# The MLP of the last 1024 tokens as a 2x2 block product with seven products

## The chip, the cores and the metric

The kernel runs on one core of a Trainium2 chip. A core has TensorE (PE, the matrix unit), VectorE (DVE), ScalarE (ACT), GpSimd (POOL) and SyncE (SP). Here SP issues all data transfers (DMA) from one queue, in order; each engine takes its own instructions in order too, and waits for the others by semaphores. Operands lie in SBUF (128 partitions); TensorE adds up into PSUM, which has eight banks of 128x512 float32. The metric is the device time of one execution in microseconds, lower is better. Before the change it is 2673.2 us (median of 3 runs, 2673.03 to 2673.42).

## The reference

One layer on 2048 tokens of width 1024: two token mixers (attention and a state-space scan), a mixing projection that gives `h`, and then the MLP, which is all that the change touches:

```python
hn = rmsnorm(h, norm2_g)
a = jnp.square(jax.nn.relu(hn @ w_mlp_in.astype(jnp.float32)))   # 1024 -> 4096
h = h + a @ w_mlp_out.astype(jnp.float32)                        # 4096 -> 1024
```

## The kernel before

Tokens are kept reversed in time and cut into quarters of 512. Activations are kept with features on the partitions and tokens along the row, so a matmul has a 128x128 piece of a weight as its stationary operand and 128 features x 512 tokens as its moving one. Every float32 operand is split into a high part (rounded to the matmul's type `float32r`, a copy on ScalarE) and a low part (the difference, a subtraction on VectorE); `mm3` then issues three matmuls per pair: high x high, high x low, low x high. This splitting is the `split` of weights, activations and `hn`.

The program is a set of generators ("streams") that are run side by side, weighted by estimated cost; a scheduler then fixes the order of each engine's instructions when the program is built, with a model of its own for the times. The stages are: input projection and state space; attention; then for the quarters at tokens 1536 and 1024 the mixing projection and the MLP of that quarter (`mlp_stream` with 512 tokens, here called the quarter MLP); beside the second quarter MLP runs `mix_stream` for the last 1024 tokens in blocks of 256 ("mix2"), which writes `hS` (the residual) and `hnS` (the normed input, already split) to DRAM. The last stage is `mlp_stream` with 1024 tokens: this is the stage that is replaced.

In that stage, for each of the 32 chunks of 128 hidden features (`f`) and both halves of the tokens (`th`), `mlp1` makes 8 x 3 matmuls into one PSUM bank, ScalarE takes relu and square, VectorE splits the result, and the chunk's two halves wait as `a`. After each pair of chunks `mlp2` makes, for each of 8 output blocks and both token halves, 2 x 3 matmuls, and VectorE adds the bank to the residual `acc` in SBUF. Four `mlp2` units follow each `mlp1` unit. That is 64 times (24 + 24) = 3072 matmuls. `hn` and `acc` come from DRAM once; each chunk's `w1` and `w2` rows (512 KB each) are loaded and split once. After the last chunk each finished block of `acc` goes to `out`.

Of the kernel before, what the change touches and what calls it, by code (L numbers as in the profile page):

```python
# [31 lines left out]
for _n, _w in (("g1", 8), ("qg", 1), ("kg", 1), ("lre", 32), ("lim", 32), ("ldt", 32),  # L32
# [13 lines left out]
    "hnS": (2, 2, 128, 8, QT),  # L46
}

# [10 lines left out]
class Kern:  # L59
# [5 lines left out]
    # ---------------------------------------------------------------- helpers  # L65
# [18 lines left out]
    def mm3(self, ps, lh, ll, rh, rl, start, stop):  # L84
        mm = self.nc.tensor.matmul
        mm(ps, lh, rh, start=start, stop=False)  # L86
        mm(ps, lh, rl, start=False, stop=False)  # L87
        mm(ps, ll, rh, start=False, stop=stop)  # L88
# [9 lines left out]
    # ---------------------------------------------------------------- constants  # L98
# [18 lines left out]
    # ---------------------------------------------------------------- projection  # L117
# [174 lines left out]
    # ---------------------------------------------------------------- attention  # L292
# [155 lines left out]
    # ---------------------------------------------------------------- SSM parameters  # L448
# [62 lines left out]
    def ssm_params(self):  # L511
# [24 lines left out]
        # coefficient of b: (lam_bar - 1) / lam  # L536
# [18 lines left out]
        # powers of lam_bar, both orders  # L555
# [18 lines left out]
        # rho^8  # L574
# [4 lines left out]
        # signed unit phasors of 8 theta * 2^k  # L579
# [27 lines left out]
    # ---------------------------------------------------------------- SSM  # L607
# [8 lines left out]
    def ssm_stream(self):  # L616
# [15 lines left out]
        # phasor tables  # L632
# [46 lines left out]
        def tables(st, q):  # L679
# [21 lines left out]
            # input matrices  # L701
# [11 lines left out]
            # output matrices  # L713
# [142 lines left out]
    # ---------------------------------------------------------------- GLU, mixing, norms  # L856
# [155 lines left out]
    def mix_tail(self, X, b):  # L1012
# [23 lines left out]
    # ---------------------------------------------------------------- MLP  # L1036
    def mlp_stream(self, es, blocks, TB, p_hn, ps1, ps2, side="left", held=None):
# [3 lines left out]
        NT = TB // 512  # L1041
# [6 lines left out]
        p_acc = tp("acc", 1)  # L1048
# [13 lines left out]
        for t0 in blocks:  # L1062
            qs = list(range(t0 // QT, (t0 + TB) // QT))
            for q in qs:
                yield ("need", f"hn{q}")
            w1, w2, av, hn, acc = {}, {}, {}, {}, {}
            raw1 = {0: load("w1", 0)}
            for k in range(8):
                for x in range(2):
                    if held:  # L1070
                        hn[k, x] = held[0][k][:, x]
                        continue
                    t = p_hn.tile([128, TB], F32R, tag=f"hn{k}{x}", name=f"hn{k}{x}")
                    for i, q in enumerate(qs):
                        nc.sync.dma_start(out=t[:, i * QT:(i + 1) * QT].bitcast(F32), in_=S["hnS"][q, x, :, k, :])
                    hn[k, x] = t
            raw1[1] = load("w1", 1)
            w1[0] = split(raw1.pop(0), p_w1, "w1")
            raw2 = load("w2", 0)

            def mlp1(f, th):
                ps = ps1.tile([128, 512], F32, tag="m", name="m1")
                w = w1[f]
                sl = slice(th * 512, th * 512 + 512)
                for k in range(8):
                    self.mm3(ps, w[:, 0, k * 128:(k + 1) * 128], w[:, 1, k * 128:(k + 1) * 128],
                             hn[k, 0][:, sl], hn[k, 1][:, sl], k == 0, k == 7)
                r = p_r.tile([128, 512], F32, tag="r", name="r")
                nc.scalar.activation(out=r, in_=ps, func=ACTF.Relu)  # L1089
                nc.scalar.activation(out=r, in_=r, func=ACTF.Square)  # L1090
                if th == 0:
                    av[f] = p_a.tile([128, 2, TB], F32R, tag="a", name="a")
                a = av[f]
                nc.vector.tensor_copy(out=a[:, 0, sl], in_=r)
                tt(nc.vector, a[:, 1, sl], r, a[:, 0, sl].bitcast(F32), ALU.subtract)

            def mlp2(f0, o, th):
                ps = ps2.tile([128, 512], F32, tag="m", name="m2")
                sl = slice(th * 512, th * 512 + 512)
                for i in range(2):  # L1100
                    w, a = w2[f0 + i], av[f0 + i]
                    self.mm3(ps, w[:, 0, o * 128:(o + 1) * 128], w[:, 1, o * 128:(o + 1) * 128],
                             a[:, 0, sl], a[:, 1, sl], i == 0, i == 1)
                tt(nc.vector, acc[o][:, sl], acc[o][:, sl], ps, ALU.add)
# [175 lines left out]
```

## Time and profile before

| | |
|---|---|
| runs: median (lowest to highest) | 2673.2 us (2673.03 to 2673.42) |
| profiled execution: span from first to last instruction | 2671.6 us |
| last stage: first matmul on `hn` to end of the last matmul | 1958.5 to 2667.7 us |
| TensorE busy over the span | 2546.3 us (95%) |
| VectorE, ScalarE, GpSimd busy | 73%, 46%, 37% |
| mean granted TensorE clock | 0.978 |

The profiler recorded one execution; no time of its own for that execution beyond the span is shown, and the median of the runs is 1.6 us above the span. In the profile's rows, L73 is the helper that issues every two-operand elementwise operation, and L86 to L88 are the three matmuls of `mm3`. Matmuls are pipelined: a row's duration is about 0.39 us, while the next one starts about 0.23 us after it, so starts are what count. `x` is a count, and what stands behind the second bar is idle time ahead of the instructions and what ended it.

### The profile page before, as it was taken

To read this page: it belongs to the slowest core of one execution; us is meant where nothing else is said; L and a number is where in the kernel's file an instruction comes from. 1 tells how busy PE (TensorE), PEld (TensorE's weight loads), DVE (VectorE), ACT (ScalarE), POOL (GpSimd) and SP (SyncE) were. 2 spreads that over 40 slices of the span, in tenths; PEclk is the share of its full clock that TensorE was granted. 3 is DMA by queue.
4 is the path that set the end of the run, shared out by engine and by line. 5 is a ranking of instruction groups with operands and counts; after the bars stand their busy time and mean duration, and the time that the engine had idled before them with its cause. 6 is when DMAs were issued, how large, how long until landed. Compare 5 with 4: busy or idle time off the path is not lost.

```text
span 2671.6 us, 35510 instructions
## 1 busy us (share of the span) xinstructions
PE 2546.3 (95%) x12368; PEld 2096.5 (78%) x12368; DVE 1945.6 (73%) x2790; ACT 1216.8 (46%) x2193; POOL 990.3 (37%) x898
## 2 busy tenths in 40 slices
PE   8888889988899999999898999999999999999999
PEld 6776677876778888888686788888888888888887
DVE  7699997888998888988999876767644444444443
ACT  6444446765666566655665554444321121212120
POOL 5685766866865444544675312122000000000000
PEclk9999999999999999999998999999999999999999
DMA  8545448774443333333433355555651111111101
GB/s 290 189 122 158 134 147 245 201 211 122 140 122 108 120 116 104 120 108 105 135 108 98 101 174 164 196 190 170 236 189 40 55 40 56 40 56 40 56 26 70
DMA packets 247588, 340.66 MB, mean 128 GB/s; under 512 B 23280, under 2 KB 157168, under 8 KB 247408
## 3 DMA queue, kind: packets, MB, share of 16 engines
q1 hardware_dynamic: 247408, 338.38, 40.7%
q8 instruction: 98, 1.61, 0.2%
q14 instruction: 82, 0.67, 0.1%
HBM read 278.40 MB, written 58.72 MB: 126 GB/s over the span
## 4 chain that ended last, share of the span: by engine, by line
PE 68%; DVE 4%; issue 1%; ACT 1%; POOL 0%; DMA 0%; DVEq 0%; ACTq 0%; POOLq 0%
PE m L86 20%; PE m L88 20%; PE m L87 19%; PE at L389 3%; PE z L349 3%; PE o L409 2%; PE o L408 2%; DVE C L373 1%; DVE lo L73 1%; DVE h L73 1%; DVE w L73 0%; DVE hs L1023 0%; ACT s L364 0%; DMA w<-in_w_dram 0%; ACT a L365 0%
## 5 line engine op out<-in xcount | busy, mean ns | idle before, releaser
L73 POOL TENSOR_TENSOR a<-a,C 128x512 f32<-128x512 f32 (+1 forms) x320 | 463.7, 1459 | 362.3 <-DVE C L373 131.5
L73 DVE TENSOR_TENSOR acc<-acc,m 128x512 f32<-128x512 f32 x256 | 174.7, 684 | 391.0 <-PE m L88 387.2
L86 PE MATMUL m<-a,w 128*128 128x512 f32 x1024 | 402.9, 394 | 0.3 <-DVE h L73 0.3
L87 PE MATMUL m<-a,w 128*128 128x512 f32 x1024 | 399.6, 390 | 0.0
L88 PE MATMUL m<-a,w 128*128 128x512 f32 x1024 | 399.5, 392 | 0.0
L88 PE MATMUL m<-h,w 128*128 128x512 f32 (+1 forms) x992 | 357.3, 362 | 8.2 <-DVE w L73 8.1
L86 PE MATMUL m<-h,w 128*128 128x512 f32 (+1 forms) x992 | 358.8, 365 | 2.7 <-ACT w L905 1.4
L87 PE MATMUL m<-h,w 128*128 128x512 f32 (+1 forms) x992 | 358.0, 362 | 3.2 <-DVE h L73 3.1
L1089 ACT ACTIVATE r<-m 128x512 f32<-128x512 f32 x128 | 76.8, 600 | 599.3 <-PE m L88 599.1
L373 DVE TENSOR_TENSOR_SCAN C<-s,C,mz 128x513 f32<-128x513 f32 x192 | 273.5, 1440 | 15.2 <-ACT s L364 6.7
L73 DVE TENSOR_TENSOR w<-w,w 128x1024 fp32r<-128x1024 f32 x192 | 249.5, 1318 | 47.4 <-ACT w L1058 45.1
L364 ACT ACTIVATE s<-z 128x512 f32<-128x512 f32 (+1 forms) x320 | 172.2, 540 | 153.9 <-PE z L349 149.2
L1058 ACT ACTIVATE w<-w 128x1024 fp32r<-128x1024 f32 x192 | 198.8, 1057 | 91.3 <-PE m L88 68.5
L393 ACT ACTIVATE hi<-at 128x512 fp32r<-128x512 f32 (+1 forms) x320 | 170.3, 541 | 133.1 <-PE at L389 119.0
L88 PEld LDWEIGHTS m<-a,w 128*128 128x128 f32 x1024 | 192.2, 188 | 41.8
L86 PEld LDWEIGHTS m<-a,w 128*128 128x128 f32 x1024 | 192.3, 188 | 40.2 <-DVE h L73 0.9
L87 PE MATMUL m<-w,x 128*128 128x512 f32 x512 | 210.5, 411 | 13.9 <-DVE w L154 13.7
L87 PEld LDWEIGHTS m<-a,w 128*128 128x128 f32 x1024 | 192.4, 188 | 39.7
L86 PE MATMUL m<-w,x 128*128 128x512 f32 x512 | 209.5, 412 | 14.3 <-ACT w L153 7.4
L73 DVE TENSOR_TENSOR h<-h,m 128x512 f32<-128x512 f32 x256 | 170.2, 674 | 69.3 <-PE m L88 68.7
L73 DVE TENSOR_TENSOR lo<-at,hi 128x512 fp32r<-128x512 f32 (+1 forms) x320 | 185.3, 594 | 46.3 <-ACT hi L393 45.0
L88 PEld LDWEIGHTS m<-h,w 128*128 128x128 f32 x992 | 189.6, 191 | 37.1 <-DVE w L73 10.4
(211 smaller groups left out, 5418.4 us busy)
## 6 DMA issues: line engine op xcount, KB each, us to landing
w<-in_w_dram SPq DMA_DIRECT2D x192, 512.0 KB, 3.6
wr<-in_w_in_dram SPq DMA_DIRECT2D x104, 256.0 KB, 3.9
k<-kS SPq DMA_DIRECT2D x160, 128.0 KB, 3.5
v<-vS SPq DMA_DIRECT2D x80, 256.0 KB, 3.1
wr<-in_w_out_dram SPq DMA_DIRECT2D x40, 512.0 KB, 4.1
xr<-in_xt_dram SPq DMA_DIRECT2D x31, 512.0 KB, 4.3
xn<-in_xn_dram SPq DMA_DIRECT2D x16, 512.0 KB, 5.9
vS<-v SPq DMA_DIRECT2D x16, 512.0 KB, 4.1
```

The costliest lines, as they stand in the source:

```text
L73: eng.tensor_tensor(out=out, in0=a, in1=b, op=op)
L86: mm(ps, lh, rh, start=start, stop=False)
L87: mm(ps, lh, rl, start=False, stop=False)
L88: mm(ps, ll, rh, start=False, stop=stop)
L349: nc.tensor.matmul(z[:, i0:512], qt[g, h][m][:, u * 128:(u + 1) * 128], kt[b][:, i0:512], start=(m == 0), stop=(m == 1))
L364: nc.scalar.activation(out=s1[:, 1 + i0:513], in_=z[:, i0:512], func=ACTF.Sigmoid, scale=-0.125)
L373: nc.vector.tensor_tensor_scan(out=C[:, 0:513], data0=s1[:, 0:513], data1=self.mz[:, 128:641], initial=self.C[(n - 4) % 6][:, 512:513], op ...
L389: nc.tensor.transpose(at[:, u * 128:(u + 1) * 128], at_a[b, u][:, kb * 128:(kb + 1) * 128], self.ident)
L393: nc.scalar.activation(out=hi[:, :n], in_=at[:, :n], func=ACTF.Copy)
L408: nc.tensor.matmul(o[:, :n], vt[b][:, kb, :], hi[:, :n], start=first, stop=False)
L1058: nc.scalar.activation(out=w[:, 0], in_=raw, func=ACTF.Copy)
L1089: nc.scalar.activation(out=r, in_=ps, func=ACTF.Relu)
```

## The change

The last 1024 tokens are two blocks of 512 tokens. With features also cut in two, each of the two projections is a 2x2 block product, which is now made with seven block products (Strassen's method in Winograd's form) in place of eight. Both projections are no longer interleaved: all of the up projection comes first, its result goes through DRAM (`aS`), then the down projection.

- mix2 stores `hn` unsplit (one DMA in place of two, no split).
- `fast_types` makes the seven combinations of `hn` blocks (four plain differences or sums, three plain blocks) and splits them. Four of them (`TB11`, `TT1`, `TT2`, `TT3`) are made early, beside the end of the quarter MLP, in a pool on the right side of SBUF; three (`TB21`, `TB22`, `TT4`) when that MLP's memory is free.
- `fast_up` goes over 16 pairs of hidden chunks `i`. `fast_w1` loads four 128x512 pieces of `w1`, makes the four weight combinations and splits seven operands. Seven products of 4 x 3 matmuls go into three banks; some are added onto a bank that has been read already (`onto`). VectorE and ScalarE put the four results together, square them, and make the seven combinations for the down projection, which are stored unsplit in `aS`.
- `fast_down` goes product by product: seven products, each of 16 steps over the hidden chunks; a step makes 4 x 3 matmuls into four banks. Each step loads one 128x512 activation combination and one piece of `w2` (three pieces in the first product, `SS1`, which also makes `S2` on GpSimd and keeps it; none in the second, `SS2`), makes the weight combination where there is one, and splits both. The eight `f_raw` buffers take all of these loads. After a product's last step its banks are added to one or more blocks of the residual `C`, which is loaded from `hS` as four DMAs of 1 MB in the first step.

The core of the diff (removed text of `mlp_stream` for 1024 tokens and comment lines are left out):

```diff
-    "hnS": (2, 2, 128, 8, QT),
+    "hnS": (2, 128, 8, QT),
+    "aS": (7, 16, 128, QT),
...
-            h = self.split(X, hs)
-            hn.append(h)
-            if not X.held:
-                for x in range(2):
-                    nc.sync.dma_start(out=S["hnS"][Q, x, :, k, o0:o0 + TB], in_=h[:, x].bitcast(F32))
+            if X.held:
+                hn.append(self.split(X, hs))
+            else:
+                nc.sync.dma_start(out=S["hnS"][Q, :, k, o0:o0 + TB], in_=hs)
...
+    def hilo(self, pool, src, tag):
+        nc = self.nc
+        t = pool.tile([128, 2, 512], F32R, tag=tag, name=tag)
+        nc.scalar.activation(out=t[:, 0], in_=src, func=ACTF.Copy)
+        self.tt(nc.vector, t[:, 1], src, t[:, 0].bitcast(F32), ALU.subtract)
+        return t
...
+        for k in range(4):
+            if early:
+                b11, b12, b22 = load(0, k, "b11"), load(1, k, "b12"), load(1, k + 4, "b22")
+                t3 = stage.tile([128, 512], F32, tag="t3", name="t3")
+                self.tt(dve, t3, b22, b12, ALU.subtract)
+                self.tt(dve, b12, b12, b11, ALU.subtract)
+                keep(TB11, k, b11)
+                self.tt(dve, b22, b22, b12, ALU.subtract)
+                keep(TT1, k, b12)
+                keep(TT2, k, b22)
+                keep(TT3, k, t3)
+            else:
+                b21, b22 = load(0, k + 4, "b21"), load(1, k + 4, "b22")
+                keep(TB21, k, b21)
+                keep(TB22, k, b22)
+                t2 = ty[TT2, k].bitcast(F32)
+                t4 = stage.tile([128, 512], F32, tag="t4", name="t4")
+                self.tt(dve, t4, t2[:, 0], t2[:, 1], ALU.add)
+                self.tt(dve, t4, b21, t4, ALU.subtract)
+                keep(TT4, k, t4)
...
+            product(X, SA11, TB11, False)
+            p1 = out("p1")
+            nc.scalar.activation(out=p1, in_=X, func=ACTF.Copy)
...
+            product(Y, SS2, TT2, False)
+            u2 = out("u2")
+            tt(dve, u2, p1, Y, ALU.add)
...
+            product(Z, SS1, TT1, False)
...
+            product(Y, SS3, TT3, True)
+            u3 = out("u3")
+            tt(dve, u3, p1, Y, ALU.add)
+            v22 = out("v22")
+            tt(dve, v22, u3, Z, ALU.add)
+            nc.scalar.activation(out=v22, in_=v22, func=ACTF.Relu)
+            square(v22)
+            store(TB22, v22)
...
+            product(X, SA12, TB21, True)
...
+            product(Z, SS4, TB22, True)
...
+            product(Y, SA22, TT4, True)
...
+        order = [(SS1, TT1), (SS2, TT2), (SS3, TT3), (SS4, TB22), (SA11, TB11), (SA12, TB21), (SA22, TT4)]
...
+            if st == SS1:
+                a21, a22, a11 = quarter(i, 1, 0), quarter(i, 1, 1), quarter(i, 0, 0)
+                s1 = temp(a21, a22, ALU.add, "s1")
+                s2[i] = p_s2.tile([128, 512], F32, tag=f"s2_{i}", name="s2")
+                tt(nc.gpsimd, s2[i], s1, a11, ALU.subtract)
+                src = s1
+            elif st == SS2:
+                src = s2[i]
+            elif st == SS3:
+                src = temp(quarter(i, 1, 1), s2[i], ALU.subtract, "s3")
+            elif st == SS4:
+                src = temp(quarter(i, 0, 1), s2[i], ALU.subtract, "s4")
+            else:
+                src = quarter(i, *{SA11: (0, 0), SA12: (0, 1), SA22: (1, 1)}[st])
+            return self.hilo(self.f_hl, src, "hl")
...
+            prep(j + 1)
+            w, a = ready.pop((n, i))
+            for o in range(4):
+                c = slice(o * 128, (o + 1) * 128)
+                self.mm3(banks[o], w[:, 0, c], w[:, 1, c], a[:, 0], a[:, 1], i == 0, i == NP - 1)
+            if C is None:
+                C = {}
+                for th in range(2):
+                    for d in range(2):
+                        C[d, th] = p_h.tile([128, 4, 512], F32, tag=f"c{d}{th}", name="c")
+                        nc.sync.dma_start(out=C[d, th], in_=S["hS"][Q + th, :, 4 * d:4 * d + 4, :])
+                V = p_h.tile([128, 4, 512], F32, tag="v", name="v")
...
+                ps = (ps3, self.pool(el, "ps5b", 5, PSUM))
+                self.f_raw, self.f_hl = self.pool(el, "fraw", 8), self.pool(el, "fhl", 8)
+                self.f_s = self.pool(el, "fs", 1)
```

More of the change, by code (lines that the diff above doesn't have):

```diff
@@ L45 @@
     "hS": (2, 128, 8, QT),
-    "hnS": (2, 2, 128, 8, QT),
-}
+    "hnS": (2, 128, 8, QT),
+    "aS": (7, 16, 128, QT),
+}
+SA11, SA12, SA22, SS1, SS2, SS3, SS4 = range(7)
+TB11, TB21, TB22, TT1, TT2, TT3, TT4 = range(7)
 LN2_HI = 0.693359375
@@ L1034, in mix_tail, with mlp_stream @@
             self.flags.add(f"hn{Q}")
[L1037 removed]
+    def mlp_stream(self, es, t0, ps1, ps2, held, side="left"):
         nc, S, A = self.nc, self.S, self.A
@@ new lines, in mlp2 @@
+        def mlp2(f0, o):
+            ps = ps2.tile([128, 512], F32, tag="m", name="m2")
+            for i in range(2):
+                w, a = w2[f0 + i], av[f0 + i]
+                self.mm3(ps, w[:, 0, o * 128:(o + 1) * 128], w[:, 1, o * 128:(o + 1) * 128],
+                         a[:, 0], a[:, 1], i == 0, i == 1)
+            tt(nc.vector, acc[:, o, :], acc[:, o, :], ps, ALU.add)
+        todo = []
+        for f in range(NF):
+            if f + 2 < NF:
+                raw1[f + 2] = load("w1", f + 2)
+            if f + 1 < NF:
+                w1[f + 1] = split(raw1.pop(f + 1), p_w1, "w1")
+            mlp1(f)
+            yield mc
+            for _ in range(4):
+                if todo:
+                    mlp2(*todo.pop(0))
+                    yield mc / 4
+            w2[f] = split(raw2, p_w2, "w2")
+            if f + 1 < NF:
+                raw2 = load("w2", f + 1)
+            if f % 2 == 1:
+                todo = [(f - 1, o) for o in range(8)]
@@ new lines, in mlp_stream, with fast_types, load, keep @@
+        while todo:
+            f0, o = todo.pop(0)
+            mlp2(f0, o)
+            yield mc / 4
+            nc.sync.dma_start(out=self.out[o * 128:(o + 1) * 128, t0:t0 + 512], in_=acc[:, o, :])
+    def hilo(self, pool, src, tag):
[4 more added lines that the diff above has]
+        return t
+    def fast_types(self, stage, pool, early, ty):
+        nc, S = self.nc, self.S
+        dve = nc.vector
+        if early:
+            yield ("need", "hn1")
+            yield ("need", "hn0")
+        def load(half, k, n):
+            t = stage.tile([128, 512], F32, tag=n, name=n)
+            nc.sync.dma_start(out=t, in_=S["hnS"][half, :, k, :])
+            return t
+        def keep(t, k, src):
+            ty[t, k] = self.hilo(pool, src, f"ty{t}{k}")
+        for k in range(4):
+            if early:
+                b11, b12, b22 = load(0, k, "b11"), load(1, k, "b12"), load(1, k + 4, "b22")
[16 more added lines that the diff above has]
+                keep(TT4, k, t4)
+            yield 4.0
@@ new lines, in fast_w1, with load, temp @@
+    def fast_w1(self, i):
+        nc, A = self.nc, self.A
+        dve = nc.vector
+        def load(f, half, n):
+            t = self.f_raw.tile([128, 512], F32, tag="raw", name=n)
+            nc.sync.dma_start(out=t, in_=A["w1"][f, :, 4 * half:4 * half + 4, :].rearrange("p k t -> p (k t)"))
+            return t
+        def temp(a, b, op, n):
+            t = self.f_s.tile([128, 512], F32, tag=n, name=n)
+            self.tt(dve, t, a, b, op)
+            return t
+        hl = lambda src: self.hilo(self.f_hl, src, "hl")
+        a11, a21, a22, a12 = load(i, 0, "a11"), load(i + 16, 0, "a21"), load(i + 16, 1, "a22"), load(i, 1, "a12")
+        yield
+        w = {SA11: hl(a11)}
+        s1 = temp(a21, a22, ALU.add, "s1")
+        s2 = temp(s1, a11, ALU.subtract, "s2")
+        yield w
+        w[SS2] = hl(s2)
+        s3 = temp(a11, a21, ALU.subtract, "s3")
+        yield w
+        w[SS1] = hl(s1)
+        s4 = temp(a12, s2, ALU.subtract, "s4")
+        yield w
+        for t, src in ((SS3, s3), (SA12, a12), (SS4, s4), (SA22, a22)):
+            w[t] = hl(src)
+            yield w
```

264 lines of the change are left out of this document (176 added, 88 removed).

## The prediction

> **What bounds the kernel now.** I read the page first, for the span and the engines' shares, then the replaced stage alone: a table by windows, the chain of waits and the timeline.
>
> ```profile
> span 2671.6 us, 35510 instructions
> PE 2546.3 (95%) x12368; PEld 2096.5 (78%) x12368; DVE 1945.6 (73%) x2790; ACT 1216.8 (46%) x2193; POOL 990.3 (37%) x898
> ```
>
> The window row below lies inside the stage (length; busy time and count of PE, PEld, DVE, ACT, POOL; clock; DMA share; GB/s).
>
> ```profile
> 2008.86:2485.30 476.44, 476.44 (x2066) 387.17 (x2065) 203.57 (x301) 92.56 (x129) 0.00 (x0) 1.00 0.15 48
> ```
>
> TensorE is busy all of the time at full clock; VectorE 43%, ScalarE 19%, and DMA moves 48 GB/s. The stage is bound by its matmuls alone. Three pieces of the chain (start, length, what), one per 48 matmuls, give their rate:
>
> ```profile
> 2031.02 0.24 PE m L86
> 2042.10 0.24 PE m L86
> 2053.18 0.24 PE m L86
> ```
>
> The distance is 11.08 us, so 64 such parts take 64 x 11.08 = 709.1 us, or 230.8 ns per matmul. The timeline (start, length) has the stage's two ends and both kinds of matmul:
>
> ```profile
> 1958.54 0.40 PE L86 MATMUL m<-hn,w 128*128 128x512 f32 x1
> ...
> 2299.76 0.39 PE L87 MATMUL m<-a,w 128*128 128x512 f32 x1
> ...
> 2302.03 0.39 PE L88 MATMUL m<-a,w 128*128 128x512 f32 x1
> 2302.26 0.40 PE L86 MATMUL m<-hn,w 128*128 128x512 f32 x1
> ...
> 2305.99 0.39 PE L87 MATMUL m<-hn,w 128*128 128x512 f32 x1
> ...
> 2667.44 0.39 PE L88 MATMUL m<-a,w 128*128 128x512 f32 x1
> ...
> 2667.86 0.69 DVE L73 TENSOR_TENSOR acc<-acc,m 128x512 f32<-128x512 f32 x1 [0.67 <-PE m L88]
> ```
>
> From 1958.54 to 2667.67 are the same 709.1 us. Ten distances on `a` are 2.27 us, 227.0 ns each; sixteen on `hn` are 3.73 us, 233.1 ns each. Behind the last matmul lie one add and the last store, 3.8 us to the end of the span.
>
> **The change part by part: matmuls.** Up and down are 16 x 7 x 12 = 1344 matmuls each, 2688 in place of 3072. At 227.0 ns they take 610.2 us, at 233.1 ns 626.6 us. Why `hn` runs slower no row tells; it lies on the right side of SBUF, as the four early combinations do. I take 227.0 ns for 1920 matmuls and the middle, 230.1, for the 768 on early combinations: 435.8 + 176.7 = 612.5 us, 96.6 less than now. What remains is to count the waits that the new stage brings. It has 652 VectorE instructions (20 x 16 and 20 in up, 312 in down) where there were 448 (7 per 48 matmuls), and loads everything just ahead of use.
>
> Prices of one operation: groups of the stage (count, busy, mean ns, idle before), GpSimd's from the whole span, two VectorE rows that start 0.59 us apart, and transfers (count, KB, us to landing).
>
> ```profile
> L73 DVE TENSOR_TENSOR a<-r,a 128x512 fp32r<-128x512 f32 x59 | 40.6, 688 | 1.1
> L1090 ACT ACTIVATE r<-r 128x512 f32<-128x512 f32 x59 | 37.1, 628 | 1.0
> ```
>
> ```profile
> L73 POOL TENSOR_TENSOR a<-a,C 128x512 f32<-128x512 f32 x224 | 363.9, 1634 | 338.6 <-DVE C L373 131.5 <-ACT a L365 113.8 <-ACT s L364 16.8
> ```
>
> ```profile
> 1901.72 0.68 DVE L73 TENSOR_TENSOR h<-h,m 128x512 f32<-128x512 f32 x1
> 1902.31 0.68 DVE L73 TENSOR_TENSOR a<-r,a 128x512 fp32r<-128x512 f32 x1
> ```
>
> ```profile
> hn<-hnS SPq DMA_DIRECT2D x26, 256.0 KB, 6.0
> out_dram<-h SPq DMA_DIRECT2D x6, 256.0 KB, 3.3
> wr<-in_w_glu_dram SPq DMA_DIRECT2D x14, 256.0 KB, 2.9
> ```
>
> So a VectorE operation on 128x512 takes 0.69 us, or 0.60 in a row of independent ones; a high part on ScalarE 0.63; GpSimd's subtraction 1.63; a 256 KB load lands after 2.9 us, in a burst after 6.0.
>
> **Before the stage.** mix2 loses its split and one store of two. TensorE has no idle time there, so I cost the relief at nothing. Early combinations add 28 VectorE operations beside the quarter MLP:
>
> ```profile
> 1900.00:1957.00 57.00, 56.67 (x251) 46.60 (x250) 32.66 (x46) 14.02 (x18) 0.00 (x0) 1.00 0.71 255
> ```
>
> 32.7 + 28 x 0.60 = 49.5 of 57 us: covered, but that MLP has only three banks, and an add that stands behind others holds TensorE. 0 to 4 us; I take 1.
>
> **The opening.** On TensorE, before, the last matmuls of the quarter MLP (`m2`) are followed at once by those on `hn`:
>
> ```order
> L86 MATMUL m2_19927<-a_19826,w2_19861 128x512
> L87 MATMUL m2_19927<-a_19826,w2_19861 128x512
> L88 MATMUL m2_19927<-a_19826,w2_19861 128x512
> L86 MATMUL m1_20027<-hn00_19967,w1_20017 128x512
> L87 MATMUL m1_20027<-hn01_19970,w1_20017 128x512
> ```
>
> Now the same place (`fx`, `fy` banks, `ty` combinations, `hl` split weights):
>
> ```order
> L92 MATMUL m2_19884<-a_19783,w2_19818 128x512
> L90 MATMUL fx_20031<-ty00_18473,hl_19994 128x512
> L91 MATMUL fx_20031<-ty00_18473,hl_19994 128x512
> L90 MATMUL fy_20032<-ty40_18480,hl_20001 128x512
> L91 MATMUL fy_20032<-ty40_18480,hl_20001 128x512
> L92 MATMUL fx_20031<-ty00_18473,hl_19994 128x512
> ```
>
> Only two matmuls stand ahead of `hl_20001`. That tile lies where the quarter MLP's residual lay, so its high part waits for that residual's last add and store: 0.69 + 3.3 + 0.63 = 4.6 us, less two matmuls (0.45): 4.2 us idle. At least the four ScalarE copies queued there, 2.5 us; at most, with a store like a burst load, about 8.
>
> Does the gap slow the clock? One place shows it: rows of the timeline with the idle time before them, and windows after.
>
> ```profile
> 1429.17 1.12 PE L888 MATMUL m<-ident,rc 128*128 128x128 f32 x4 [3.55 <-POOL rc L73]
> ...
> 1436.58 0.44 PE L389 MATMUL at<-ident,a 128*128 128x128 f32 x2 [1.42 <-DVE lo L73]
> ```
>
> ```profile
> 1430.00:1434.00 4.00, 4.00 (x15) 3.33 (x14) 4.00 (x3) 2.29 (x5) 2.75 (x3) 0.50 0.22 89
> 1434.00:1438.00 4.00, 2.07 (x8) 1.03 (x7) 4.00 (x5) 3.98 (x8) 1.48 (x2) 0.93 0.47 131
> 1438.00:1442.00 4.00, 3.65 (x11) 3.06 (x12) 4.00 (x6) 1.68 (x5) 2.09 (x2) 0.59 0.15 33
> ```
>
> After 3.55 us the clock was 0.50 for 4 us, a loss of 2 us. Here 0 to 2; I take 1.
>
> **Up projection.** Late combinations are 20 more VectorE operations within the first two blocks: (20 + 40) x 0.60 = 36 us beside 168 matmuls of 38.8. Just covered; 0 to 5, I take 2. A later block has 20 VectorE operations (12.0 us), 16 on ScalarE (10) and 11 transfers of 256 KB beside 84 matmuls of 19.3 us. All hidden on average; but banks are written again after VectorE has read them, and a queue out of step costs up to one operation or two. 0 to 1 us per block; I take 0.25, so 4 us for 16.
>
> **From up to down.** On SP, the middle of the old stage held only weights:
>
> ```order
> L1053 DMA w1_20728<-in_w1_dram 128x1024
> L1053 DMA w1_20863<-in_w1_dram 128x1024
> L1053 DMA w2_20861<-in_w2_dram 128x1024
> L1053 DMA w2_20996<-in_w2_dram 128x1024
> L1053 DMA w1_20998<-in_w1_dram 128x1024
> ```
>
> At the turn of the new one stand the residual's four 1 MB loads, ahead of what step 2 of `SS1` needs (`ar_22630`, its activations):
>
> ```order
> L1223 DMA aS_65<-v11_22497 128x512
> L1350 DMA c_22608<-hS_63 128x2048
> L1350 DMA c_22610<-hS_63 128x2048
> L1350 DMA c_22612<-hS_63 128x2048
> L1350 DMA c_22614<-hS_63 128x2048
> L1320 DMA ar_22630<-aS_65 128x512
> L1293 DMA w2_22647<-in_w2_dram 128x512
> ```
>
> `c` takes memory of early combinations, which are free only near the end of up; from there to step 2 TensorE has 49 matmuls, 11.3 us. How fast loads go shows a window with a burst of `hn` loads, and the page's densest slice below that, its first:
>
> ```profile
> 1910.00:1920.00 10.00, 10.00 (x46) 8.29 (x45) 4.64 (x7) 1.22 (x2) 0.00 (x0) 1.00 1.04 388
> ```
>
> ```profile
> GB/s 290 189 122 158 134 147 245 201 211 122 140 122 108 120 116 104 120 108 105 135 108 98 101 174 164 196 190 170 236 189 40 55 40 56 40 56 40 56 26 70
> ```
>
> 4.19 MB at 388 GB/s are 10.8 us, then 2.9 for `ar` and 1.3 for its split: 15.0, so step 2 comes 3.7 us late (at 290 GB/s, 7.4; 0 if memory comes free early). The Trainium skill ("DMA: Bandwidth & Descriptors", Specifications) gives a core about 358 GB/s of HBM; by that the wait would be an estimated 4.6 us. The window of 388 speaks against it, and I go by the window.
>
> **Down projection.** A step is 12 matmuls, 2.76 us. VectorE's rows in `SS1` are per step (`s1` the combination, `hl` low parts), where the old stage had one add per 6 matmuls:
>
> ```order
> L77 TENSOR_TENSOR s1_22773<-w2_22767,w2_22769 128x512
> L77 TENSOR_TENSOR hl_22777<-s1_22773,hl_22777 128x512
> L77 TENSOR_TENSOR hl_22782<-ar_22780,hl_22782 128x512
> L77 TENSOR_TENSOR s1_22803<-w2_22797,w2_22799 128x512
> L77 TENSOR_TENSOR hl_22807<-s1_22803,hl_22807 128x512
> ```
>
> The second waits for ScalarE between: 0.69 + 0.63 + 0.60 + 0.60 = 2.5 us a step, just under TensorE, in `SS3` and `SS4` too (0 to 3 us, I take 0). `SS1` alone also loads 1.05 MB a step: 2.7 us at 388 GB/s, 3.6 at 290. With both so near I take 3.0: 13 steps x 0.24 = 3.1 us (0 to 11). The other products load half or a quarter of it, four steps ahead. At the products' ends 4 to 12 adds of 0.69 us stand between splits; the banks alternate, and 12 adds (8.3 us) with the splits of three steps (3.6) beside four steps (11) leave about 1 us late, as 8 do after `SS1`: 2 us together (0 to 5). The tail is the old one: four banks end 0.7 us apart, one add, one store.
>
> **Sum.** Waits: 1 + 4.2 + 1 + 2 + 4 + 3.7 + 3.1 + 2 = 21.0. Span: 2671.6 - 709.1 + 612.5 + 21.0 = 2596.0. The median lies 1.6 above the profiled span, so 2598 us, 75 less than 2673.2.
>
> **The rivals.** *Loads set the pace.* For: in a burst 256 KB landed after 6.0 us, and in `SS1` a buffer is used again every second step: 6.0 + 0.69 + 1.63 = 8.3 us per two steps, 4.2 a step, 13 x 1.4 = 18 in place of 3.1; with 1 us per block of up (16 for 4) and 7.4 for 3.7 that is 31 more: 2629. Against: `hn` kept 388 GB/s in such a burst.
>
> *Nothing waits but the opening.* 610.2 us of matmuls and 2.5: 2598 - 2.3 - 18.5 = 2577. For: VectorE's averages fit everywhere. Against: the order of loads at the turn.
>
> *Short waits keep the clock down, and it is slower.* If each step of down waits a little for a split, TensorE is never idle for long, yet the window at 1438 shows 0.59 after a gap of 1.42 us. Down's 1344 matmuls take 305 us at full clock; at a mean clock of 0.80 they take 76 more, which eats the whole gain; at 0.67, the mean of those three windows, 150 more: 2748. Against: no row of down's work is longer than a step, and the eight buffers let steps be made ahead. The Trainium skill ("TensorE: Matmul & The Clock Gate", the part on the clock gate) has the clock halved only after an idle window of about 3.4 us. By that rule, gaps of 1 us in each step change nothing; the 0.50 after 3.55 us agrees, the 0.59 after 1.42 does not.
>
> That the change doesn't do what it says is excluded for the matmuls: TensorE's rows are 384 fewer.
>
> **How the numbers follow.** Chances: forecast 0.76, loads 0.13, nothing waits 0.07, clock 0.04. The likeliest gives 2598. With every wait at its low end it is 2577, with every one at its high end (and 626.6 of matmuls) 2653; all at once is unlikely. From 2582 to 2634 lie the forecast and most of the loads case. 0.2% (5 us) is about what a measurement of this kernel tells from no change; only the clock case reaches beyond 2668, partly: faster 0.95, same 0.01, slower 0.04.
>
> **What would show it.** Right: the new stage about 634 us from the quarter MLP's last matmul; one idle time of some 4 us at the opening and one of 3 to 4 at step 2 of `SS1`; matmuls 227 to 233 ns apart; clock 1.00 but for these places. Wrong: idle time in every step of `SS1`, `SS3` or `SS4`, VectorE full in up, or a clock below 0.9 over a whole product.

## The result and the profile after

The changed kernel takes 2605.3 us (median of 4 runs, 2604.1 to 2611.1) against 2673.3 (4 runs): a ratio of 0.9749, 95% interval 0.9735 to 0.9763. The forecast was 2598 us, range 2582 to 2634: right side, inside the range, 7.3 us too low. The profiled execution is the longest of the four; its earlier stages ran some 4 us later than in a second profile of the same kernel (`after_again`, below), so the last stage is compared from its own first wait or its own start.

The page of the changed kernel, for the same two lines as before:

```profile
span 2609.4 us, 36346 instructions
PE 2471.2 (95%) x11984; PEld 2030.9 (78%) x11984; DVE 2069.8 (79%) x2990; ACT 1360.0 (52%) x2481; POOL 1023.4 (39%) x922
```

TensorE has 384 rows fewer and 75 us less of busy time; its share is still 95%, so the page alone does not tell that there is anything new to find. The windows do (length; busy time and count of PE, PEld, DVE, ACT, POOL; clock; DMA share; GB/s), from the opening to the turn into down:

```profile
1966.50:1970.80 4.30, 0.95 (x4) 0.36 (x3) 3.79 (x6) 2.45 (x6) 0.00 (x0) 1.00 0.66 209
1970.80:1974.40 3.60, 3.60 (x10) 2.78 (x11) 3.01 (x5) 3.60 (x8) 0.00 (x0) 0.55 0.34 116
2010.00:2280.00 270.00, 269.92 (x1167) 218.62 (x1166) 174.19 (x271) 126.70 (x222) 1.30 (x1) 1.00 0.44 151
2288.00:2292.00 4.00, 0.88 (x4) 0.38 (x3) 2.67 (x4) 0.01 (x1) 0.00 (x0) 1.00 0.95 342
2292.00:2296.00 4.00, 2.76 (x7) 2.21 (x8) 1.85 (x3) 1.26 (x2) 1.14 (x1) 0.50 1.03 389
2320.00:2330.00 10.00, 9.80 (x39) 6.50 (x38) 7.66 (x11) 3.58 (x6) 3.90 (x3) 1.00 0.99 337
```

Up (the third row) is solid: 1167 matmuls in 270 us, 231.4 ns each, nothing idle. Two short stretches stand almost empty, each with a stretch at half clock behind it. The last row, in `SS1`, is the one to look at twice: TensorE is "busy" 9.80 of 10 us, yet only 39 matmuls started, where 44 fit at 227 ns. A matmul's row is 0.39 us long and the next starts 0.23 us after it, so a start that slips by up to 0.16 us leaves no idle time. The count shows it; the busy share and the list of waits do not. That list, for TensorE from 1850 us on (total, times, longest):

```profile
PE g L90 <- ACT hl L1117: 7.7, 4, 4.4
PE m L90 <- DVE h L77: 2.8, 4, 1.4
PE fy L90 <- ACT hl L1117: 1.7, 1, 1.7
PE fx L90 <- ACT hl L1117: 1.6, 1, 1.6
PE g L91 <- DVE hl L77: 1.3, 1, 1.3
```

From the starts of all matmuls in the trace the stage divides as follows. "Free" is what the matmuls alone would take: 1344 x 231.4 ns in up, 227 ns in down; nine matmuls of `SS1` stand among the last ones of up, because the compiled order puts them there.

```
part                                       measured   free   more
last m2 to first fx                            1.99   0.23    1.8
first fx to last fz (up, 9 of SS1)           316.84  313.0    3.8
to the first matmul of SS2                    57.50   41.5   16.0
SS2                                           43.57   43.5    0.1
SS3 to the end of SA22                       219.17  217.6    1.6
stage                                        639.07  615.8   23.3
```

### The profile page after: what moved, and what is told of

Its sections match the earlier page's. It is cut to its first block, busy times and chain, and to the rows that moved or that the text cites. A ratio compares the mean times of both kernels' runs of the same rounds, so it can differ in the third digit from the quotient of the medians.

```text
span 2609.4 us, 36346 instructions
## 1 busy us (share of the span) xinstructions
PE 2471.2 (95%) x11984; PEld 2030.9 (78%) x11984; DVE 2069.8 (79%) x2990; ACT 1360.0 (52%) x2481; POOL 1023.4 (39%) x922
## 4 chain that ended last, share of the span: by engine, by line
PE 63%; DVE 6%; DMA 3%; issue 2%; ACT 1%; POOL 0%; SPq 0%; DVEq 0%; ACTq 0%; POOLq 0%
PE m L90 10%; PE m L92 10%; PE m L91 10%; PE g L91 3%; PE g L92 3%; PE z L353 3%; PE g L90 3%; PE at L393 3%; PE o L413 2%; PE o L412 2%; PE fy L90 2%; PE fy L91 2%; PE fy L92 2%; DVE C L377 1%; DMA w<-in_w_dram 1%
## 5 line engine op out<-in xcount | busy, mean ns | idle before, releaser
L91 PE MATMUL m<-w,x 128*128 128x512 f32 x512 | 210.9, 412 | 14.7 <-DVE w L158 14.5
L90 PE MATMUL m<-w,x 128*128 128x512 f32 x512 | 208.9, 411 | 14.8 <-DVE v L260 6.1
L90 PEld LDWEIGHTS m<-h,w 128*128 128x128 f32 x992 | 189.3, 191 | 34.9 <-ACT w L909 3.0
L92 PEld LDWEIGHTS m<-h,w 128*128 128x128 f32 x992 | 189.4, 191 | 34.3 <-DVE w L77 7.6
L91 PEld LDWEIGHTS m<-h,w 128*128 128x128 f32 x992 | 189.8, 192 | 29.7 <-DVE h L77 4.0
L92 PE MATMUL m<-w,x 128*128 128x512 f32 x512 | 208.3, 407 | 0.5 <-DVE x L77 0.5
L90 PE MATMUL m<-a,w 128*128 128x512 f32 x512 | 202.4, 396 | 2.2 <-DVE h L77 2.1
L91 PE MATMUL m<-a,w 128*128 128x512 f32 x512 | 200.4, 392 | 0.0
L92 PE MATMUL m<-a,w 128*128 128x512 f32 x512 | 200.1, 393 | 0.0
L77 DVE TENSOR_TENSOR w<-w,w 128x1024 fp32r<-128x1024 f32 x128 | 172.9, 1368 | 31.3 <-ACT w L1059 28.4
L77 POOL TENSOR_TENSOR s<-s,w 128x512 f32<-128x512 f32 x16 | 20.7, 1296 | 438.0 <-PE fx L92 376.3
L393 PE MATMUL at<-ident,a 128*128 128x128 f32 x1088 | 179.2, 281 | 4.6 <-POOL a L77 3.3
L91 PE MATMUL g<-hl 128*128 128x512 f32 x448 | 176.6, 394 | 1.9 <-DVE hl L77 1.3
```

What stands on the lines that cost most here:

```text
L77: eng.tensor_tensor(out=out, in0=a, in1=b, op=op)
L90: mm(ps, lh, rh, start=start, stop=False, skip_group_check=onto)
L91: mm(ps, lh, rl, start=False, stop=False, skip_group_check=onto)
L92: mm(ps, ll, rh, start=False, stop=stop, skip_group_check=onto)
L393: nc.tensor.transpose(at[:, u * 128:(u + 1) * 128], at_a[b, u][:, kb * 128:(kb + 1) * 128], self.ident)
```

## The experiments

The three questions: what the first 5.6 us cost, what makes `SS1` 16.0 us long, and why up's matmuls are slower than down's. Ratios are to the kernel before, with runs of it on the same chip; parts of the stage are counted as above.

### c_late: the residual's loads out of the turn

```diff
-            if C is None:
+            if n == 1 and i == 1:
                 C = {}
...
+                        tt(dve, C[d, th][:, 0, 0:1], s2[15][:, 0:1], s2[15][:, 0:1], ALU.add)
                         nc.sync.dma_start(out=C[d, th], in_=S["hS"][Q + th, :, 4 * d:4 * d + 4, :])
...
+            if n == 1 and i == 9:
+                for o in range(4):
+                    for d in range(2):
+                        tt(dve, C[d, 1][:, o, :], C[d, 1][:, o, :], held[o], ALU.add)
...
-                    add(C[0, 1])
-                    add(C[1, 1])
+                    held = banks
```

The small add in front of each load reads the last kept `s2`, so the load can't start before `SS1` has its operands; the banks of `SS1` are added to `C` in the tenth step of `SS2`.

> The residual's four 1 MB loads are held back until the last S2 of the first down product is made, and the first product's banks are added to it in the middle of the second product. If the bytes of these loads delay step 2 of the first product (my theory), the idle times of 4.4 and 1.6 us there and the low clock behind them (about 1.8 us) go: about 2598 us, 7 less than the changed kernel. Rival: step 2 waits for the store and load of its activations through DRAM or for SP's queue, whatever lies between: idle time as before, 2604 to 2606.

2600.9 us (2597.1 to 2603.9), ratio 0.9731 (0.9716 to 0.9746). In the changed kernel the turn read (SyncE's queue; start, length of the issue):

```profile
2277.91 2.08 SPq L1350 DMA_DIRECT2D c<-hS  x4
2280.08 0.53 SPq L1320 DMA_DIRECT2D ar<-aS  x1
```

```profile
c<-hS SPq DMA_DIRECT2D x4, 1024.0 KB, 8.8
```

```profile
2288.50 0.39 PE L92 MATMUL g<-hl 128*128 128x512 f32 x1
2293.24 0.80 PE L90 MATMUL g<-hl 128*128 128x512 f32 x1 [4.36 <-ACT hl L1117]
```

`ar`, the activations of a step, is issued behind the four `c` loads, which land after 8.8 us; TensorE stands still for 4.36 us. With the loads moved, the windows of the same times have no empty stretch and full clock:

```profile
2288.00:2292.00 4.00, 4.00 (x19) 3.30 (x19) 3.31 (x4) 1.15 (x2) 1.61 (x1) 1.00 1.05 399
2292.00:2296.00 4.00, 3.29 (x15) 2.26 (x13) 3.81 (x7) 1.11 (x2) 1.12 (x1) 1.00 0.99 344
```

The part up to `SS2` falls from 57.50 to 49.32 us: the loads' place costs 8.2 (7.6 against the 56.93 of the kernel's second profile). In the changed kernel these are the gap of 4.36, a second of 1.59 two steps later (its load stood behind stores of up's results), and twelve matmuls 0.43 us apart between them, at half clock, 2.4 us. The remaining 7.8 us over the free time are steps of 3.0 to 4.4 us in place of 2.72.

### s2_on_vector: S2 taken from GpSimd

```diff
-                tt(nc.gpsimd, s2[i], s1, a11, ALU.subtract)
+                tt(dve, s2[i], s1, a11, ALU.subtract)
```

> The first product's S2 is made on VectorE in place of GpSimd. If a step's 3.13 us there comes from the low part that takes 1.15 us beside GpSimd's subtraction (my theory), a step falls to 2.76 to 2.8 us, TensorE's own, though VectorE has one operation more: 13 x 0.35 = 4.6 us less, about 2600 us. Rival: the loads set it (1.05 MB per 3.13 us are 335 GB/s): steps stay at 3.1 us, 2605.

2603.1 us (2601.9 to 2612.4), ratio 0.9747 (0.9727 to 0.9768): the time hardly moves. The groups of `SS1` (2290 to 2340 us) in the changed kernel, then here:

```profile
L77 POOL TENSOR_TENSOR s<-s,w 128x512 f32<-128x512 f32 x13 | 16.8, 1295 | 35.6 <-DVE s L77 26.3 <-DMA aS<-v 9.3
L77 DVE TENSOR_TENSOR hl<-s,hl 128x512 fp32r<-128x512 f32 x13 | 15.1, 1161 | 10.1 <-ACT hl L1117 10.1
```

```profile
L77 DVE TENSOR_TENSOR hl<-s,hl 128x512 fp32r<-128x512 f32 x13 | 9.0, 692 | 0.6
L77 DVE TENSOR_TENSOR s<-w,w 128x512 f32<-128x512 f32 x13 | 9.0, 691 | 6.0 <-DMA w<-in_w_dram 5.9
```

The low part of the weight takes 692 ns in place of 1161 once GpSimd is idle, but then VectorE waits 5.9 us for `w`: another limit stands right behind the one removed.

### opening: other memory for the first split weights

```diff
-                self.f_raw, self.f_hl = self.pool(el, "fraw", 8), self.pool(el, "fhl", 8)
-                self.f_s = self.pool(el, "fs", 1)
+                self.f_hl, self.f_v = self.pool(el, "fhl", 8), self.pool(el, "fv", 1)
+                self.f_raw, self.f_s = self.pool(el, "fraw", 8), self.pool(el, "fs", 1)
                 with ExitStack() as eu:
-                    self.f_v = self.pool(eu, "fv", 1)
```

> The split weights get other memory, so that none lies where the quarter MLP's residual lay. If the second split weight waits for that residual's last store (my theory), the idle 3.4 us at the opening and about 1.8 us of low clock go: about 2600 us. Rival: the opening is bound by VectorE, which has the late combinations to split; the wait then moves a few us on, to the first late combination: 2604 to 2606.

2602.6 us (2600.9 to 2605.6), ratio 0.9742 (0.9725 to 0.9758). The changed kernel's opening, then this one's:

```profile
1966.27 0.39 PE L92 MATMUL m<-a,w 128*128 128x512 f32 x1
1968.26 0.50 PE L90 MATMUL fx<-ty,hl 128*128 128x512 f32 x1 [1.60 <-ACT hl L1117]
...
1970.74 0.50 PE L90 MATMUL fy<-ty,hl 128*128 128x512 f32 x1 [1.75 <-ACT hl L1117]
```

```profile
1958.98 0.39 PE L92 MATMUL m<-a,w 128*128 128x512 f32 x1
1959.20 0.40 PE L90 MATMUL fx<-ty,hl 128*128 128x512 f32 x1
```

The first matmul follows at once, which gives 1.8 us, and the second wait and the half clock are gone too. The two waits had different causes, which ScalarE's rows in the changed kernel show:

```profile
1966.02 1.15 ACT L1117 ACTIVATE ty<-b 128x512 fp32r<-128x512 f32 x2 [10.45 <-DVE h L77]
1967.07 0.61 ACT L1117 ACTIVATE ty<-t 128x512 fp32r<-128x512 f32 x1
1967.59 0.61 ACT L1117 ACTIVATE hl<-a 128x512 fp32r<-128x512 f32 x1
1970.06 1.67 ACT L1117 ACTIVATE hl<-s 128x512 fp32r<-128x512 f32 x3 [1.85 <-DVE t L77]
```

The first split weight (`hl<-a`) stood in ScalarE's queue behind three copies of late combinations (`ty`): that is the first wait. The edit also changed the compiled order: in `opening` this copy starts at 1948.19, ahead of them, so the first 1.8 us are the queue's and not shown to be the memory's. The second split weight (`hl<-s`) lies where the residual lay, and in the program its copy waits for the residual's last add, over at 1967.4, and for the stores, the last of which was issued at 1967.4 and landed 2.3 us later. (The row puts the wait down to a VectorE operation that ended at much the same time; the program has no such wait.) So the second wait was for that memory, as the prediction had it.

But up takes 0.4 us longer than before (317.28). Its first block of 84 matmuls is 3.7 us shorter (19.56 us), its second and fourth together 3.0 longer, its last 1.0 longer. VectorE, which has the late combinations to make, is full in the first block, as this window of `opening` shows, and TensorE waits for it in the second:

```profile
1959.20:1978.76 19.56, 19.56 (x85) 15.75 (x84) 19.56 (x34) 10.06 (x19) 0.00 (x0) 1.00 0.67 222
```

For this part the rival came: the second wait moved on to the late combinations. The stage is 2.9 us shorter: 1.8 less the 0.4, and another 1.6 that lie between up and `SS2`, where four steps behind a second gap of 2.84 us kept to 2.72 to 2.78 us; that part differs by 0.6 us between two runs of the changed kernel.

### fourth_matmul: are the products bound by their matmuls?

```diff
-                self.mm3(banks[o], w[:, 0, c], w[:, 1, c], a[:, 0], a[:, 1], i == 0, i == NP - 1)
+                self.mm3(banks[o], w[:, 0, c], w[:, 1, c], a[:, 0], a[:, 1], i == 0, i == NP - 1 and n < 4)
+                if n >= 4:
+                    nc.tensor.matmul(banks[o], w[:, 1, c], a[:, 1], start=False, stop=i == NP - 1)
```

Low x low is added in the last three products: 192 matmuls more.

> In the last three down products each step gets a fourth matmul per bank (low x low): 192 more matmuls and no more loads or splits. If matmuls set the pace there (my theory), 192 x 0.227 = 43.5 us more: about 2649 us. Rival: loads or splits set it and TensorE has room: at most 10 us more, 2615.

2647.7 us (2644.9 to 2649.7), ratio 0.9906 (0.9891 to 0.9921), 42.4 us above the changed kernel. In the trace the last five products take 261.1 in place of 219.2 us, 41.9 more; 192 x 226.7 ns are 43.5, less the 1.6 us that the changed kernel loses there at a product's end, which a longer step hides. So down behind `SS2` is bound by matmuls alone.

### late_and_opening, all_three and the control

`late_and_opening` has both edits, `all_three` also S2 on VectorE; `after_again` is the changed kernel once more, on the same chip.

> The four residual blocks are loaded in the second product in place of the first, SS1's own adds to them follow there, and the buffers of the high and low parts and of the results are taken from SBUF ahead of the raw ones at the opening. Counted from the first wait beside the quarter MLP to the last matmul, the late residual alone took 690.5 us and the opening alone 695.6, the changed kernel 698.7. If the two are separate costs they add up: about 687.4 us, a time about 11 us below the changed kernel where the run is free of drift, 2594 to 2599 us. Rival: what the opening gives is given back at the turn (its waits there were 4.04 and 2.84 us against 4.36 and 1.59), so that with the turn relieved only the late residual counts: 690.5 us, 2598 to 2601.

> As late_and_opening, and SS1's S2 is also made on VectorE in place of GpSimd. Theory: in SS1 two limits lie close together. With GpSimd busy, VectorE's subtraction hl<-s,hl takes 1.16 us in place of 0.69 and the step takes 3.13 us; without it, the steps wait for loads of w, but there the burst of the residual's loads still stood in the way. With both taken away, a step needs five VectorE operations (3.4 us at 0.69, but 3.0 at 0.60 in a row) and 1 MB of loads (2.7 us at 388 GB/s): between 2.8 and 3.1 us in place of 3.13, so 0 to 4 us below late_and_opening. Rival: the loads alone set 3.1 us at the 338 GB/s of this stretch, and nothing is gained.

> The changed kernel once more, on the same chip as the three others: 2605 us, and in its profile no late start of the last stage: from the first wait beside the quarter MLP to the last matmul 698.7 us as before, while that first wait comes at about 1902 us in place of 1906.45, if the 8 us that the stage began late in its first profile were a drift of that run.

```
                   us (lowest to highest)        ratio (95%)             stage   up     to SS2
after_again        2606.4 (2603.3 to 2609.0)   0.9744 (0.9731-0.9757)  639.03  316.93  56.93
late_and_opening   2594.8 (2591.8 to 2599.1)   0.9702 (0.9689-0.9715)  628.60  316.68  49.01
all_three          2596.6 (2591.2 to 2597.9)   0.9704 (0.9690-0.9717)  628.93  316.25  49.68
```

The control's stage is the same to 0.04 us and begins 4 us earlier than in the first profile: that lateness was the run's. The two costs are separate: the loads' place gives 8.2 us of the stage, the opening 2.3 on top of it; the medians lie 11.6 apart. From the first wait beside the quarter MLP to the last matmul `late_and_opening` takes 687.7 us, as expected. `all_three` gains nothing. VectorE there makes four operations a step (not the five of the expectation), and between 2295 and 2325 us it stood idle five times, 5.2 us in all, each time for a piece of `w`: the loads alone hold `SS1` as much as GpSimd does. Whether by their rate (318 GB/s there) or because a load starts only when VectorE has given a buffer back, no run separates.

### fewer_loads and a11_in_second: which limit holds SS1

Both stand on `late_and_opening`. `fewer_loads` leaves a load out and keeps GpSimd's operation (its `S2` is then another matrix); `a11_in_second` relieves both, with S1 kept and S2 made in `SS2`.

```diff
-                a21, a22, a11 = quarter(i, 1, 0), quarter(i, 1, 1), quarter(i, 0, 0)
+                a21, a22 = quarter(i, 1, 0), quarter(i, 1, 1)
+                a11 = a21
```

```diff
-                a21, a22, a11 = quarter(i, 1, 0), quarter(i, 1, 1), quarter(i, 0, 0)
-                s1 = temp(a21, a22, ALU.add, "s1")
                 s2[i] = p_s2.tile([128, 512], F32, tag=f"s2_{i}", name="s2")
-                tt(nc.gpsimd, s2[i], s1, a11, ALU.subtract)
-                src = s1
+                tt(dve, s2[i], quarter(i, 1, 0), quarter(i, 1, 1), ALU.add)
+                src = s2[i]
             elif st == SS2:
                 src = s2[i]
+                tt(dve, src, src, quarter(i, 0, 0), ALU.subtract)
```

> On top of late_and_opening: SS1's third load is left out and its second operand is taken from the first piece, so S2 and with it the output are others; GpSimd still makes S2. If GpSimd's work beside VectorE alone can hold SS1 at 3.1 us per step, the pace stays at 3.1 and hl<-s,hl at 1.1 us (687 us from the first wait to the last matmul). If the loads are what holds it, as in all_three, and VectorE's slower subtraction only fills idle time, the pace falls to 2.72 us (682 us).

> On top of late_and_opening: the third piece of w2 of each step is loaded in SS2 in place of SS1, and S2 is made there on VectorE, in place of the kept S1. SS1 then has three loads per step (768 KB) and three VectorE operations, SS2 two loads, and GpSimd has nothing. Theory: SS1's steps of 3.13 us had two limits close together, VectorE slowed by GpSimd's S2 and the loads of 1 MB per step; with both taken away its matmuls set the pace, 48 x 0.0567 = 2.72 us per step, and 13 steps give back 5.3 us: 682.4 us from the first wait beside the quarter MLP to the last matmul, against 687.7; 2589 to 2592 us. Rival: a third limit (ScalarE's copies in a chain with VectorE) keeps 3.1 us; or SS2, beside the loads of the residual, now waits in its turn: 687 us, no gain.

2591.9 us (2590.5 to 2599.3; 0.9698, 0.9679 to 0.9716) and 2595.5 (2591.4 to 2597.3; 0.9703, 0.9687 to 0.9720). The same ten microseconds of `SS1` in `late_and_opening`, `all_three`, `fewer_loads` and `a11_in_second`:

```profile
2310.00:2320.00 10.00, 9.76 (x40) 6.73 (x39) 7.30 (x10) 3.88 (x8) 4.38 (x4) 1.00 0.93 317
```

```profile
2310.00:2320.00 10.00, 8.33 (x36) 6.14 (x35) 8.25 (x13) 3.46 (x6) 0.00 (x0) 1.00 0.94 315
```

```profile
2310.00:2320.00 10.00, 9.81 (x40) 6.71 (x39) 7.66 (x10) 4.07 (x9) 4.10 (x4) 1.00 0.79 250
```

```profile
2310.00:2320.00 10.00, 10.00 (x46) 8.29 (x45) 7.76 (x16) 4.73 (x9) 0.00 (x0) 1.00 0.93 290
```

In the first two the pace is alike on the mean whichever engine makes S2, though not in these ten microseconds (40 and 36 matmuls): the steps from the fifth on take 3.3 and 3.4 us. With DMA down to 79% and GpSimd still at work there are 40 matmuls as before; these steps take 3.15 us, and the part up to `SS2` 46.93 in place of 49.01 (from the first wait beside the quarter MLP to the last matmul 685.7 us, between the two expected values). `a11_in_second` has the same three loads and the same three VectorE operations in a step of `SS1` and differs there by GpSimd's operation: so GpSimd alone can hold the pace, and the loads add a little. With both relieved there are 46 matmuls, every step of `SS1` but the first is 2.72 us, and the part up to `SS2` takes 43.07. The expected 5 us of gain still went elsewhere: at the end of up the compiled order has three matmuls of `SS1` in place of nine, and TensorE waited for `p` there:

```profile
2265.34 0.39 PE L92 MATMUL fy<-ty,hl 128*128 128x512 f32 x1
2267.80 0.50 PE L90 MATMUL fx<-ty,hl 128*128 128x512 f32 x1 [2.07 <-ACT p L1227]
```

Up grew from 316.7 to 318.9 with six matmuls fewer in it, and `SS2`, now with loads beside the residual's, from 43.5 to 45.9. The stage is 1.3 us shorter, the time the same: the rival's outcome, with the mechanism of the theory.

How GpSimd holds a step is seen in the changed kernel's timeline (VectorE, GpSimd):

```profile
2323.40 0.68 DVE L77 TENSOR_TENSOR s<-w,w 128x512 f32<-128x512 f32 x1
2324.86 1.15 DVE L77 TENSOR_TENSOR hl<-s,hl 128x512 fp32r<-128x512 f32 x1 [0.78 <-ACT hl L1117]
2325.93 0.68 DVE L77 TENSOR_TENSOR hl<-ar,hl 128x512 fp32r<-128x512 f32 x1
2326.53 0.68 DVE L77 TENSOR_TENSOR s<-w,w 128x512 f32<-128x512 f32 x1
...
```

```profile
2324.16 1.30 POOL L77 TENSOR_TENSOR s<-s,w 128x512 f32<-128x512 f32 x1 [1.83 <-DVE s L77]
```

GpSimd starts as soon as `s` is there and ends at 2325.46; VectorE's subtraction begins at 2324.86 and ends at 2326.01, 0.55 us behind GpSimd's end. The same 0.55 us come out in every step from 2305 us on, as if it got its turn only at that end. From one `s` to the next are 3.13 us. The Trainium skill ("SBUF — State Buffer", "SBUF: two separate sides") says that a VectorE operation with two SBUF inputs and a GpSimd operation that reads SBUF exclude each other for the whole instruction; this timing agrees. VectorE's adds from PSUM (`c<-c,g`) beside GpSimd's adds kept their 0.67 us.

### halves_in_turn: the waits beside the quarter MLP

On top of `a11_in_second`:

```diff
-                b11, b12, b22 = load(0, k, "b11"), load(1, k, "b12"), load(1, k + 4, "b22")
+                b12, b22, b11 = load(1, k, "b12"), load(1, k + 4, "b22"), load(0, k, "b11")
                 t3 = stage.tile([128, 512], F32, tag="t3", name="t3")
                 self.tt(dve, t3, b22, b12, ALU.subtract)
+                keep(TT3, k, t3)
...
-                keep(TT3, k, t3)
```

> a11_in_second, and the early combinations begin with those of the second token half (TT3), whose input was stored a block earlier; the ones that need the last block's stores come behind them. In the changed kernel ScalarE stood 10.06 us and VectorE 5.67 us for the first load of hn, with the quarter MLP's copies and adds queued behind, and TensorE lost 1.34 + 0.66 + 0.35 us. If the last store is what all waited for, these 2.4 us mostly go: about 2 us below a11_in_second. Rival: the wait only moves, since the operation on the last block still stands ahead of the MLP's on both engines: no difference that can be measured.

2595.8 us (2592.8 to 2600.6), ratio 0.9711 (0.9693 to 0.9730): the rival. Waits of TensorE there (1895 to 1920 us) in `after_again`, and here:

```profile
PE m L90 <- DVE h L77: 2.4, 3, 1.3
```

```profile
PE m L90 <- ACT r L1076: 1.7, 1, 1.7
PE m L90 <- DVE h L77: 0.4, 1, 0.4
```

The wait moved from VectorE's adds to ScalarE's copies; both queues still have a combination of the last block ahead of the MLP's work.

### act_right and act_left: does the place of the moving operand set its rate?

The split activations of down get a pool of four buffers of their own, on the right side of SBUF or on the left:

```diff
+        p_act = self.pool(es, "fact", 4, None, "right")
...
-            return self.hilo(self.f_hl, raw, "hl")
+            return self.hilo(p_act, raw, "ac")
```

> The split activation operands of the down projection are placed in a pool of their own on the right side of SBUF; nothing else is changed. If the place of the moving operand sets its rate (matmuls on hn before and on the early combinations now, all on the right side, start 0.2333 us apart, others 0.227), the 1344 matmuls of down take 0.0063 us longer each: about 8.5 us more, 2614 us. If the slower rate in up has another cause (VectorE's and ScalarE's accesses beside it, the weight's buffers), down stays at 0.227 us and the time within 2 us of the changed kernel.

> As act_right, a pool of four buffers of their own for the down projection's split activations, but on the left side. act_right's matmuls in down started 0.2334 us apart in place of 0.2268. If the place did that, they start 0.2268 us apart here and the time is that of the changed kernel, 2604 to 2607 us, give or take its turn (whose waits change with the number of buffers: act_right's came to 5 us more). If it was the smaller pool, with operands prepared later and VectorE and ScalarE working at other moments of the matmuls, they start 0.233 us apart here too, 2612 to 2615 us.

2614.3 us (2610.8 to 2616.9; 0.9772, 0.9759 to 0.9785) and 2611.4 (2607.8 to 2613.9; 0.9763, 0.9742 to 0.9784). A stretch of down in which TensorE never waits, in `after_again`, `act_right`, `act_left`:

```profile
2400.00:2500.00 100.00, 100.00 (x443) 82.81 (x442) 65.79 (x105) 43.20 (x76) 0.00 (x0) 1.00 0.62 195
```

```profile
2400.00:2500.00 100.00, 100.00 (x430) 80.35 (x429) 64.81 (x101) 42.63 (x73) 0.00 (x0) 1.00 0.60 187
```

```profile
2400.00:2500.00 100.00, 100.00 (x443) 82.81 (x442) 66.77 (x104) 43.88 (x75) 0.00 (x0) 1.00 0.62 194
```

443 matmuls per 100 us on the left with either pool, 430 on the right, at the same full clock: the place does it, and not the smaller pool. `act_left` is slow for another reason: its pool opens only when up's memory is free, and TensorE stands 13.7 us at the turn. `act_right` loses at its turn too (63.6 us to `SS2` in place of 56.93), so that its time came out at the expected 2614 is partly chance; the count is the evidence.

What it is about the place stays open. In the program built from `act_right` the four buffers begin at bytes 139232 to 151520 of a partition, and two left-side parts of up's `TB22` and `TT4` at 142016 and 146112, between them: these took 226.7 and 226.8 ns, the four buffers 233.3. So the address by itself does not decide. All moving operands of `mm3` on the right side begin 32 bytes off a multiple of 64, all on the left on a multiple of 64, before the change too. No run has one without the other, so this offset is a rival to the side that was not tested.

## Why the prediction was right, and where it was not

The stage was forecast at 632.5 us from the quarter MLP's last matmul (its 634 counts the early combinations' 1 us too) and took 639.0. Term by term:

- **Matmuls**, 612.5 forecast, 615.7 measured (311.0 in up, 304.7 in down). The count and down's 227 ns were right. In up the four early combinations took 233.1 to 233.6 ns, so the full rate that `hn` had shown applied and the middle, 230.1, was the wrong choice; `act_right` and `act_left` show that the place of the operand is the cause (its side, or its start off a multiple of 64 bytes). Of the three combinations on the left, plain `TB22` took 226.7, the others 229.2 and 230.1; why is open.
- **Opening and clock**, 5.2 forecast, 5.6 measured (1.60 + 1.75 idle and half clock behind it). The size came out, the reason in part: the second wait was for the residual's memory, but the first was ScalarE's queue of copies, which the prediction had only as the low end of its range, and half clock cost about 2 where 1 was allowed.
- **Late combinations and up's steady waits**, 2 and 4 forecast, nothing seen. For the steady blocks VectorE's averages were enough: the second to the fifteenth took 19.4 to 19.5 us, their matmuls alone. The late combinations were made in part while TensorE lost its 5.6 us at the opening; in `opening`, without that head start, they cost the second and fourth block 3.0 us, so this term was not empty but hidden.
- **The residual's loads**, 3.7 forecast. The first gap, 4.36 us, was of that size and in that place, but the term stopped at the first gap. Half clock behind it (2.4) and a second gap (1.59) were left out; with them it is 8.2 (`c_late`).
- **SS1's steps**, 3.1 forecast at 3.0 us a step, 7.8 measured at 3.1 to 3.3. This is the step that failed by its mechanism: VectorE's 2.5 us per step took 0.60 for the subtraction, from a row without GpSimd's work beside it. Beside S2 it takes 1.15. `fewer_loads` shows that this alone holds a step at 3.15; `all_three` that without it the loads hold a step at 3.4, so 3.0 was low on either account.
- **Product ends, SS3 and SS4**, 2 and 0 forecast, 1.6 and 0 measured; `fourth_matmul` shows the matmuls as the bound there.
- **Early combinations beside the quarter MLP**, 1 forecast, 2.4 of idle time measured, inside its 0 to 4.

The stage's errors are +3.2 + 0.4 - 6 + 4.5 + 4.7 - 0.4 = 6.4 us, and the early combinations add 1.4. That is about the 7.3 us by which the median missed. That the median came so near is luck in part: 6 us of waits allowed in up paid for two thirds of what was missing in `SS1`.

Of the rivals, none came. Loads did not set the pace anywhere outside `SS1`; the short slips there did not touch the clock, which the windows show at 1.00, so the case of a slower kernel had no support. Two of the prediction's signs of being wrong did show: the steps of `SS1` all started late, though with almost no idle time, and VectorE was full in up's first block.

## What to carry to other kernels

Count instructions per window beside the busy share: an engine that is 98% "busy" started 39 matmuls where 44 fit. A term for a late load has to include what comes behind the gap: the clock, and the next load that queued behind the same burst. Where two limits of a step lie within a few per cent, removing either gains nothing, and removing both shows whether the rest of the program can use the time. Work done in the shadow of a wait comes to light when the wait is removed: look for it before counting the whole wait as gain.

## What the runs showed of the hardware that was not expected

- The moving operand's place in SBUF set its rate: 226.7 ns per 512 columns on the left, 233.4 on the right (`act_left`, `act_right`), 3% for nothing else. The side and the start address (32 bytes off a multiple of 64, or on one) go together in all runs.
- VectorE's subtraction with two SBUF inputs took 1.15 us in place of 0.68 when it began inside GpSimd's operation, and ended 0.55 us behind it in every step from 2305 us on.
- The clock fell to half after shorter idle times than the 3.55 us of the kernel before. `a11_in_second` had the one gap of 2.07 us shown above, and behind it:

```profile
2268.00:2269.40 1.40, 1.40 (x6) 1.11 (x6) 1.40 (x3) 0.79 (x2) 0.00 (x0) 0.91 0.00 0
2269.40:2272.50 3.10, 3.10 (x9) 2.38 (x8) 1.65 (x3) 0.26 (x1) 0.00 (x0) 0.50 0.95 352
```

It came 1.7 us after work had begun again and lasted 3 us. Yet a gap of 2.75 us in `act_right` had no such stretch behind it, nor had single gaps of 1.65 us and less, so the length of a gap alone does not decide. The Trainium skill ("TensorE: Matmul & The Clock Gate", "What's actually happening") puts half clock after an idle window of about 3.4 us and calls the window free-running; the gap of 2.07 us speaks against the length, the two together for the second part.
